# Up projection in seven products of block sums for five of eight pairs of k-tiles, on normalised x

## The chip, the cores and the metric

The kernel runs on one core of one Trainium2 chip. The metric is the time on the device in microseconds (us) of one execution; lower is better. Three runs of the kernel before were timed.

## What is computed

One layer of a sequence model on x of 256 tokens by 2048 features, all in float32: a mixing part (attention and a recurrence, with its own projections w_in and w_out), and after it an MLP:

```
h2 = rms_norm(x, norm_mlp[l])
u = jnp.square(jax.nn.relu(jnp.einsum('btd,df->btf', h2, mlp_up[l])))
x = x + jnp.einsum('btf,fd->btd', u, mlp_down[l])
```

mlp_up is 2048 by 8192, mlp_down 8192 by 2048. rms_norm divides each token's row by the root of its mean square and multiplies by norm_mlp.

## The kernel before, in words

**Numbers.** TensorE multiplies in a reduced form of float32 (fp32r). To keep float32's accuracy each operand is split into a part `hi`, rounded to fp32r, and a part `lo`, the rest; a product is three matmuls: hi by hi, hi by lo, lo by hi. x is the stationary operand (a unit `u[:, 0]` holds hi, `u[:, 1]` lo, four k-tiles of 128 features by 256 tokens), the weights stream.

**Jobs.** Weights come in jobs of 256 rows (two k-tiles) by 512 columns, listed in `jobs` (lines 478 to 496) in the order of use. `load` (499) fetches a job to one of NRAW = 4 raw tiles through SyncE's queue. `split` (514) takes the next raw tile, has ScalarE copy it to `hi` and VectorE subtract to `lo` (three buffers each, LOOK + 1), and loads another. It runs two jobs ahead of the matmuls. `gemm` (528) goes over the jobs of one group of 512 output columns: for each job two k-tiles by two halves of 128 tokens by three matmuls of 128 rows, 128 columns of weights and 512 columns, 12 matmuls, into one PSUM bank per half; then `evac` empties the banks. Banks have two tags, "acc" and "side", of four each; up and down groups take turns between them (529).

**MLP.** `up_group` (1386) makes 512 of the 8192 hidden columns, from 8 jobs, on `hT`, which is x times norm_mlp, not yet divided by the root mean square. Its evacuation `f` (1389) does that by a scale of 1/rms per token (`rstd2`), with the relu, in 32 pieces of 32 tokens by 128, which it moves to a tile `z` in 32-blocks: EV = (8, 8) says that eight of 16 pieces of each half go to ScalarE and the others to VectorE. `fin` (1402), which is called a job or so into the next group, transposes z by blocks on VectorE, squares and rounds on ScalarE, and subtracts on VectorE: the unit of u. A down group takes the eight k-tiles of two units and 512 output columns (four jobs, 48 matmuls); `add_evac` (1342) adds it to x in two additions. `make_h` (1359) makes hT from x as it stands after w_out; `first_stats` (1425) the scale.

**Order.** Lines 1428 to 1438: up groups 0 and 1; then for each e from 0 to 7 up group 2e + 2, four down groups on units 2e and 2e + 1, up group 2e + 3 (at e = 6 both up groups come first, at e = 7 none is left). Work of the kernel is recorded, not issued: a planner (`plan`, 193) sorts the recorded operations by its own costs and dependences, gives each engine its fixed order, and takes, of what can start earliest, the one with the lowest rank; splits have their rank lowered by SPL = 120. `hooks` put recorded work between the jobs of a group. All tiles of 1040 elements a partition share NF = 18 slots of tag "f"; units have eight slots of tag "act". As every operation is issued from line 332, the profile's groups are told apart by their tiles.

Of the kernel before, what the change touches and what calls it, by code (L numbers as in the profile page):

```python
# [21 lines left out]
P = 128  # L22
T = 256
# [8 lines left out]
NF = 18  # L32
NRAW = 4
LOOK = 2
EV = (8, 8)

SPL = 120
KEEP = 0.3
# [296 lines left out]
def record(ctx, tc, A, nc):  # L335
# [28 lines left out]
    def done(n=1):  # L364
        live[0] -= n
# [113 lines left out]
    cols = [(c + 512 * h, 512) for h in range(2) for c in (4096, 3072, 5120)] + [(c + 512 * h, 512) for h in range(2) for c in (0, 1024, 2048)]  # L479
    cols.insert(1, (6144, 288))  # L480
    for c0, n in cols:
        jobs += [(A["w_in"], 256 * k, c0, n) for k in range(8)]
    for hh in range(2):
        jobs += [(A["w_out"], r0 + 512 * hh + 256 * k, 512 * j, 512) for j in range(4) for r0 in (W, 0) for k in range(2)]
    def up_jobs(i):
        return [(A["up"], 256 * k, 512 * i, 512) for k in range(8)]
# [12 lines left out]
    def load(between=None):  # L499
# [14 lines left out]
    def split():  # L514
        if pos[1] < len(jobs):
            pos[1] += 1
            raw, n = raws.popleft()
            hi = wp.tile([P, 2, 512], F32R, tag="hi", bufs=LOOK + 1, name=nm("hi"))
            lo = wp.tile([P, 2, 512], F32R, tag="lo", bufs=LOOK + 1, name=nm("lo"))
            nc.rank = -SPL  # L520
            for ks in ((slice(0, 1), slice(1, 2)) if pos[1] < 4 else (slice(0, 2),)):
                nc.scalar.copy(hi[:, ks, :n], raw[:, ks, :n])
                nc.vector.tensor_sub(lo[:, ks, :n], raw[:, ks, :n], hi[:, ks, :n])
            parts.append((hi, lo))
            nc.rank = 0
            load()

    def gemm(units, w, c0, ncols, evac, side=False, hooks={}, off=0):
        turn[0] += w is w_up or w is w_dn
        acc = [bank("side" if turn[0] % 2 else "acc") for _ in range(2)]  # L530
        nu = 4 if w is not w_out and w is not w_dn else 2
        nh = 2 * nu
        for j in range(nh):
            assert jobs[pos[2]][0] is w and jobs[pos[2]][2:] == (c0, ncols)
            pos[2] += 1
            hi, lo = parts.popleft()
            split()
            if j in hooks:
                hooks[j]()
            if side:  # L540
                pump(BD * ncols / 512, BA * ncols / 512)
            for kk in range(2):
                k = 2 * j + kk
                u = units[off + j // 2]
                for t in range(2):
                    xh = u[:, 0, k % 4, t * P:(t + 1) * P]
                    xl = u[:, 1, k % 4, t * P:(t + 1) * P]
                    o = acc[t][:, :ncols]
                    nc.tensor.matmul(o, xh, hi[:, kk, :ncols], start=(k == 0), stop=False)
                    nc.tensor.matmul(o, xh, lo[:, kk, :ncols], start=False, stop=False)  # L550
                    nc.tensor.matmul(o, xl, hi[:, kk, :ncols], start=False, stop=(k == 2 * nh - 1))
        evac(acc)

    def rsqrt_small(out, ss, scale, bias):
# [801 lines left out]
    parts2 = cst.tile([P, 2, 4], F32, name="parts2")  # L1356
    rstd2 = cst.tile([P, 2], F32, name="rstd2")

    def make_h(j):
        u = unit("hT")  # L1360
        hT.append(u)
        if j < 3:
# [51 lines left out]
    def store_evac(j):  # L1414
        def f(acc):
# [113 lines left out]
```

## Time and profile before

| what | value |
|---|---|
| median of three runs | 1206.91 us (1206.66 to 1206.95) |
| the profiled execution | 1209.2 us, of which the span is 1207.1 us |
| TensorE matmul busy | 1197.7 us, 99%, 6062 matmuls |
| weight loads busy | 961.0 us, 80% |
| VectorE busy | 853.0 us, 71% |
| ScalarE busy | 736.5 us, 61% |
| DMA | 216.08 MB, mean 179 GB/s |

The span runs from the first to the last instruction of the program on the core. PE is TensorE's matmuls, PEld its weight loads, DVE VectorE, ACT ScalarE, SP SyncE. A matmul's end is modelled, so its length in the records (395 ns for 512 columns) is more than its distance to the next; the distance of starts is what a matmul costs in a row of them. In names, out<-in are tiles of the program; x<-x,acc is the residual addition of a down group, z<-side,rstd a piece of the relu.

### The profile page before, as it was taken

Reading aid. Unit: us, or ns where it says so; the run is one execution under the profiler, and the core shown is the slowest. Engines: PE = TensorE matmul, PEld = TensorE weight load, DVE = VectorE, ACT = ScalarE, POOL = GpSimd, SP = SyncE. Lnnn points to the kernel's source line nnn. Section 1 sums busy time; section 2 is a strip of 40 time slices with the busy share of each in tenths; the row PEclk is TensorE's granted clock in tenths of the full one; section 3 lists DMA queues with packets and bytes.
Section 4 is the critical chain, followed back from the end, with each engine's and each line's share of the span. In section 5 each row is a group of like instructions: output and inputs, shape, how many; then the busy total and the mean of one; then the engine's idle time right before and its main releaser. Section 6 shows DMA issues by size and latency. Waiting matters only on the chain.

```text
span 1207.1 us, 16430 instructions
## 1 busy us (share of the span) xinstructions
PE 1197.7 (99%) x6062; PEld 961.0 (80%) x6062; DVE 853.0 (71%) x1276; ACT 736.5 (61%) x1171; POOL 7.3 (1%) x31
## 2 busy tenths in 40 slices
PE   9999999999999999999999999999999999999998
PEld 6887887878777788788888888888888888888886
DVE  7789693996965966688558568568568568567754
ACT  7774566856597769876356356356356356367532
POOL 2000000000000000000000000000000000000000
PEclk9999999999999999999999999999999999999999
DMA  8655655446554445665665665665665655666563
GB/s 282 196 171 153 184 161 164 120 139 169 155 157 155 157 151 181 180 179 184 206 175 186 198 175 190 198 180 186 203 176 186 199 174 195 195 174 199 195 204 129
DMA packets 126287, 216.08 MB, mean 179 GB/s; under 512 B 21824, under 2 KB 24384, under 8 KB 126208
## 3 DMA queue, kind: packets, MB, share of 16 engines
q1 hardware_dynamic: 126208, 215.05, 58.8%
q8 instruction: 47, 0.77, 0.3%
q14 instruction: 32, 0.26, 0.1%
HBM read 211.09 MB, written 3.93 MB: 178 GB/s over the span
## 4 chain that ended last, share of the span: by engine, by line
PE 89%; ACT 4%; DVE 3%; issue 1%; DMA 1%; SPq 0%; ACTq 0%; DVEq 0%
PE acc L332 54%; PE side L332 29%; PE tr L332 2%; PE sm L332 2%; PE sm L177 2%; ACT hi L332 1%; DVE lo L332 1%; ACT z L332 1%; DMA raw<-w_in 1%; DMA x<-xt 0%; DVE v L332 0%; ACT junk L332 0%; DVE AR L332 0%; ACT gp L332 0%; ACT L332 0%
## 5 line engine op out<-in xcount | busy, mean ns | idle before, releaser
L332 DVE TENSOR_TENSOR lo<-raw,hi 128x1024 fp32r<-128x1024 f32 (+2 forms) x395 | 474.5, 1205 | 269.6 <-ACT hi L332 267.1
L332 ACT CAST hi<-raw 128x1024 fp32r<-128x1024 f32 (+2 forms) x395 | 407.4, 1034 | 332.4 <-PE acc L332 217.5
L332 PE MATMUL acc<-hi,xT 128*128 128x512 f32 (+1 forms) x832 | 266.9, 395 | 0.5 <-ACT hi L332 0.5
L332 PEld LDWEIGHTS acc<-hi,xT 128*128 128x128 f32 x832 | 153.8, 189 | 33.9 <-ACT hi L332 2.1
L332 PE MATMUL acc<-lo,xT 128*128 128x512 f32 (+1 forms) x416 | 163.7, 393 | 0.7 <-DVE lo L332 0.5
L332 PE MATMUL acc<-hi,u 128*128 128x512 f32 x512 | 163.4, 395 | 0.0
L332 PE MATMUL side<-hi,u 128*128 128x512 f32 x512 | 163.4, 395 | 0.0
L332 PE MATMUL side<-hi,hT 128*128 128x512 f32 x512 | 162.9, 396 | 0.5 <-DVE hT L332 0.3
L332 PE MATMUL acc<-hi,hT 128*128 128x512 f32 x512 | 162.1, 395 | 0.0
L332 PEld LDWEIGHTS side<-hi,hT 128*128 128x128 f32 x512 | 96.1, 188 | 24.6 <-DVE hT L332 0.7
L332 PEld LDWEIGHTS side<-hi,u 128*128 128x128 f32 x512 | 96.1, 188 | 23.4
L332 PEld LDWEIGHTS acc<-hi,hT 128*128 128x128 f32 x512 | 96.1, 188 | 23.3
L332 PEld LDWEIGHTS acc<-hi,u 128*128 128x128 f32 x512 | 96.1, 188 | 23.3
L332 PE MATMUL acc<-lo,hT 128*128 128x512 f32 x256 | 101.1, 395 | 0.0
L332 PE MATMUL acc<-lo,u 128*128 128x512 f32 x256 | 101.1, 395 | 0.0
L332 PE MATMUL side<-lo,u 128*128 128x512 f32 x256 | 101.1, 395 | 0.0
L332 PE MATMUL side<-lo,hT 128*128 128x512 f32 x256 | 101.1, 395 | 0.0
L332 PEld LDWEIGHTS acc<-lo,xT 128*128 128x128 f32 x416 | 78.6, 189 | 18.7 <-DVE lo L332 3.1
L332 ACT ACTIVATE z<-acc,rstd 32x128 f32<-32x128 f32 x128 | 45.9, 358 | 20.1 <-DVE z L332 10.2
L332 ACT ACTIVATE z<-side,rstd 32x128 f32<-32x128 f32 x128 | 45.9, 359 | 20.1 <-DVE z L332 10.2
L332 PEld LDWEIGHTS acc<-lo,u 128*128 128x128 f32 x256 | 48.1, 188 | 11.7
L332 PEld LDWEIGHTS acc<-lo,hT 128*128 128x128 f32 x256 | 48.1, 188 | 11.7
(249 smaller groups left out, 1210.0 us busy)
## 6 DMA issues: line engine op xcount, KB each, us to landing
raw<-up SPq DMA_DIRECT2D x128, 512.0 KB, 3.8
raw<-down SPq DMA_DIRECT2D x128, 512.0 KB, 4.3
raw<-w_in SPq DMA_DIRECT2D x93, 512.0 KB, 3.8
raw<-w_out SPq DMA_DIRECT2D x32, 512.0 KB, 3.9
raw<-w_in SPq DMA_DIRECT2D x8, 288.0 KB, 3.2
x<-x SPq DMA_DIRECT2D x4, 512.0 KB, 7.5
out<-x SPq DMA_DIRECT2D x8, 256.0 KB, 3.4
raw<-w_in SPq DMA_DIRECT2D x6, 256.0 KB, 5.2
```

Of the source, the lines that this page charges most:

```text
L177: p.fn(*p.args, **p.kw)
L332: op.fn(*op.args, **op.kw)
```

## The change

For two by two blocks of matrices, seven products of sums of blocks do the work of eight (Winograd's form). The blocks here are, for a pair of k-tiles, x as two halves of tokens by two k-tiles and the weights as two k-tiles by two halves of 256 columns. In up groups 3 to 15, jobs 1, 2, 4, 5 and 7 of eight (FAST, QUICK) become fast jobs:

- Weights: `split` leaves out the lo of one block that no product uses, makes four differences of blocks T (tile `T`) on VectorE, their hi `Th` on ScalarE and their lo `Tl` on VectorE.
- x: `normal_h` makes `hN`, x times norm_mlp times 1/rms, in place of hT for groups 2 to 15, and for each of the five pairs four sums of its blocks, `S`, with hi and lo. `rstd_rows` spreads 1/rms over the partitions: two diagonal tiles and one fp32 matmul by ones.
- Matmuls: `seven` issues seven products of three matmuls of 256 columns, into four banks in place of two; the other three jobs of the group add to the first two of them.
- Evacuation: `join` adds up the four banks to a tile `C` (one copy on ScalarE, seven additions on VectorE); the relu reads C, without a scale from group 2 on. EV = 13 gives 13 of 16 pieces of each half to ScalarE.
- Order: up group 2e + 2, two down groups, up group 2e + 3, two down groups.

```diff
-EV = (8, 8)
+EV = 13
+FAST = (1, 2, 4, 5, 7)
+QUICK = 3
...
+    allone = ones[:, :1].broadcast_to([P, P])
...
+    def fast(job):
+        return job[0] is w_up and job[2] >= 512 * QUICK and job[1] // 256 in FAST
     jobs += up_jobs(0) + up_jobs(1)
     for e in range(8):
-        if e < 7:
-            jobs += up_jobs(2 * e + 2)
-        if e == 6:
-            jobs += up_jobs(15)
-        jobs += [(A["down"], e * 1024 + 256 * k, 512 * j, 512) for j in range(4) for k in range(4)]
-        if e < 6:
-            jobs += up_jobs(2 * e + 3)
+        for j in range(4):
+            if e < 7 and not j % 2:
+                jobs += up_jobs(2 * e + 2 + j // 2)
+            jobs += [(w_dn, e * 1024 + 256 * k, 512 * j, 512) for k in range(4)]
...
+                if not fast(jobs[pos[1] - 1]):
+                    nc.vector.tensor_sub(lo[:, ks, :n], raw[:, ks, :n], hi[:, ks, :n])
             parts.append((hi, lo))
+            if fast(jobs[pos[1] - 1]):
+                Tr, Th, Tl = ftile([P, 4, 256], "T"), ftile([P, 4, 256], "Th", F32R), ftile([P, 4, 256], "Tl", F32R)
+                b = raw.rearrange("p k (n c) -> p k n c", n=2)
+                nc.vector.tensor_sub(Tr[:, 0:2], b[:, :, 1], b[:, 0])
+                nc.vector.tensor_sub(Tr[:, 2], b[:, 1, 1], Tr[:, 0])
+                nc.vector.tensor_sub(Tr[:, 3], b[:, 1, 0], Tr[:, 2])
+                nc.vector.tensor_sub(lo[:, 0, :256], raw[:, 0, :256], hi[:, 0, :256])
+                nc.vector.tensor_sub(lo[:, 1], raw[:, 1], hi[:, 1])
+                nc.scalar.copy(Th, Tr)
+                nc.vector.tensor_sub(Tl, Tr, Th)
+                done()
+                parts[-1] += (Th, Tl)
...
+    def seven(acc, u, k, S, B, first, last):
+        hi, lo, Th, Tl = B
+        lt, rt = slice(0, 256), slice(256, 512)
+        def a(t, kk):
+            return [u[:, i, k + kk, t * P:(t + 1) * P] for i in range(2)]
+        def s(i):
+            return [S[:, j, i] for j in range(2)]
+        def b(kk, n):
+            return [x[:, kk, n * 256:n * 256 + 256] for x in (hi, lo)]
+        def t(i):
+            return [x[:, i] for x in (Th, Tl)]
+        for n, half, x, y in ((2, lt, a(0, 0), b(0, 0)), (0, lt, a(0, 1), b(1, 0)), (0, rt, s(3), b(1, 1)), (3, lt, s(0), t(0)),
+                              (3, rt, s(2), t(1)), (2, rt, s(1), t(2)), (1, lt, a(1, 1), t(3))):
+            o = acc[n][:, half]
+            begin = first and n > 1 and half == lt
+            end = last and (n == 1 or half == rt)
+            nc.tensor.matmul(o, x[0], y[0], start=begin, stop=False, skip_group_check=True)
+            nc.tensor.matmul(o, x[0], y[1], start=False, stop=False, skip_group_check=True)
+            nc.tensor.matmul(o, x[1], y[0], start=False, stop=end, skip_group_check=True)
...
+        quick = [j for j in range(8) if fast((w, 256 * j, c0))]
+        acc = [bank("side" if turn[0] % 2 else "acc") for _ in range(4 if quick else 2)]
...
+            if j in quick:
+                seven(acc, units[j // 2], 2 * j % 4, sums_[FAST.index(j)], (hi, lo, *T_), j == quick[0], j == quick[-1])
+                done(2)
+                continue
...
+            if keep is not None:
+                nc.scalar.copy(keep[:, 2 * kp:2 * kp + 2], b.rearrange("p (k t) -> p k t", t=T))
...
+    def rstd_rows():
+        row_rstd(rstd2, parts2)
+        dg = ftile([P, 2, P], "diag")
+        for t in range(2):
+            nc.vector.tensor_scalar(dg[:, t], ident, rstd2[:, t:t + 1], None, op0=ALU.mult)
+        b = bank("tr")
+        nc.tensor.matmul(b[:, :T], allone, dg.rearrange("p t q -> p (t q)"), start=True, stop=True)
+        done()
+        r = ftile([P, T], "r2")
+        nc.scalar.copy(r, b[:, :T])
+        rows2.append(r)
+    def normal_h(j):
+        u, a = unit("hN"), hA[j]
+        hN.append(u)
+        for kk in range(4):
+            nc.vector.scalar_tensor_tensor(a[:, kk], a[:, kk], pc("g_mlp", 4 * j + kk), rows2[0], op0=ALU.mult, op1=ALU.mult)
+        nc.scalar.copy(u[:, 0], a)
+        nc.vector.tensor_sub(u[:, 1], a, u[:, 0])
+        for p in range(2):
+            if 2 * j + p in FAST:
+                S, sr = ftile([P, 2, 4, P], "S", F32R), ftile([P, 4, P], "sr")
+                a1, a2 = a[:, 2 * p], a[:, 2 * p + 1]
+                nc.vector.tensor_add(sr[:, 0], a1[:, P:], a2[:, P:])
+                nc.vector.tensor_sub(sr[:, 1], sr[:, 0], a1[:, :P])
+                nc.vector.tensor_sub(sr[:, 2], a1[:, :P], a1[:, P:])
+                nc.vector.tensor_sub(sr[:, 3], a2[:, :P], sr[:, 1])
+                nc.scalar.copy(S[:, 0], sr)
+                nc.vector.tensor_sub(S[:, 1], sr, S[:, 0])
+                sums_.append(S)
...
+        def join(acc):
+            C, q = ftile([P, 2, 512], "C"), ftile([P, 3, 256], "q")
+            lt, rt = slice(0, 256), slice(256, 512)
+            b0, b1, b2, b3 = acc
+            nc.scalar.copy(q[:, 0], b2[:, lt])
+            nc.vector.tensor_add(q[:, 2], q[:, 0], b2[:, rt])
+            nc.vector.tensor_add(q[:, 1], q[:, 2], b3[:, lt])
+            qf = q.rearrange("p a c -> p (a c)")
+            nc.vector.tensor_add(C[:, 0], qf[:, :512], b0)
+            nc.vector.tensor_add(C[:, 1, lt], q[:, 2], b1[:, lt])
+            nc.vector.tensor_add(C[:, 1, rt], q[:, 1], b1[:, rt])
+            nc.vector.tensor_add(C[:, 1, lt], C[:, 1, lt], b3[:, rt])
+            nc.vector.tensor_add(C[:, 1, rt], C[:, 1, rt], b3[:, rt])
...
+            C = join(acc) if i >= QUICK else None
             for t in range(2):
                 for tb in range(4):
                     rows = slice(32 * tb, 32 * tb + 32)
-                    src = acc[t].rearrange("p (f c i) -> p f c i", c=4, i=32)
+                    src = (C[:, t] if C is not None else acc[t]).rearrange("p (f c i) -> p f c i", c=4, i=32)
                     for cb in range(4):
-                        o, r = z[32 * cb:32 * cb + 32, :, t, tb, :], rstd2[rows, t:t + 1]
-                        if 4 * tb + cb < EV[t]:
-                            nc.scalar.activation(o, src[rows, :, cb, :], AF.Relu, scale=r)
+                        o, s = z[32 * cb:32 * cb + 32, :, t, tb, :], src[rows, :, cb, :]
+                        r = rstd2[rows, t:t + 1]
+                        if 4 * tb + cb < EV:
+                            nc.scalar.activation(o, s, AF.Relu, **({} if i > 1 else dict(scale=r)))
+                        elif i > 1:
+                            nc.vector.tensor_scalar(o, s, 0.0, None, op0=ALU.max)
                         else:
-                            nc.vector.tensor_scalar(o, src[rows, :, cb, :], r, 0.0, op0=ALU.mult, op1=ALU.max)
+                            nc.vector.tensor_scalar(o, s, r, 0.0, op0=ALU.mult, op1=ALU.max)
...
-        gemm(hT, w_up, 512 * i, 512, f, hooks=hooks)
+        gemm(hN if i > 1 else hT, w_up, 512 * i, 512, f, hooks=hooks)
...
-    def first_stats():
-        row_rstd(rstd2, parts2)
-    up_group(0, {2: lambda: make_h(3), 4: first_stats})
-    up_group(1, {1: fin_hook})
+    up_group(0, {2: lambda: make_h(3), 4: rstd_rows})
+    up_group(1, {2 * j: lambda j=j: normal_h(j) for j in range(4)})
+    done()
     for e in range(8):
-        if e < 7:
-            up_group(2 * e + 2, {1: fin_hook})
-        if e == 6:
-            up_group(15, {1: fin_hook})
         for j in range(4):
+            if e < 7 and not j % 2:
+                up_group(2 * e + 2 + j // 2, {1: fin_hook})
             gemm(us, w_dn, 512 * j, 512, store_evac(j) if e == 7 else add_evac(x2[j]), hooks={1: fin_hook}, off=2 * e)
-        if e < 6:
-            up_group(2 * e + 3, {1: fin_hook})
```

## Rows read from the trace of the kernel before

**Rows 1.** The page's parts 1 and 2: busy time, TensorE's granted clock

```profile
PE 1197.7 (99%) x6062; PEld 961.0 (80%) x6062; DVE 853.0 (71%) x1276; ACT 736.5 (61%) x1171; POOL 7.3 (1%) x31
...
PEclk9999999999999999999999999999999999999999
```

**Rows 2.** The chain that ended last, in order of time: start us, us, what

```profile
598.12 22.40 PE acc L332 x96
...
642.92 11.20 PE acc L332 x48
```

**Rows 3.** By stretch: us, PE, PEld, DVE, ACT, POOL busy; clock, DMA, GB/s

```profile
609.32:698.92 89.60, 89.60 (x386) 72.08 (x385) 59.53 (x76) 48.75 (x68) 0.00 (x0) 1.00 0.62 188
```

**Rows 4.** VectorE in order of time, with [idle before <- releaser]

```profile
503.24 0.16 DVE L332 TENSOR_TENSOR rstd<-rsq,rsv 128x2 f32<-128x2 f32 x1
...
602.04 1.23 DVE L332 TENSOR_TENSOR lo<-raw,hi 128x1024 fp32r<-128x1024 f32 x1 [1.57 <-ACT hi L332]
```

**Rows 5.** TensorE in order of time: eight 256-column matmuls, first and last

```profile
63.25 0.28 PE L332 MATMUL tr<-XA,DA 128*128 128x256 f32 x1
...
64.08 0.28 PE L332 MATMUL tr<-XAL,DA 128*128 128x256 f32 x1
```

**Rows 6.** Groups of weight loads: busy us, mean ns | idle before

```profile
L332 PEld LDWEIGHTS acc<-hi,hT 128*128 128x128 f32 x512 | 96.1, 188 | 23.3
```

**Rows 7.** Groups of TensorE, by form: an fp32 product

```profile
L332 PE MATMUL sm<-k,q 64*128 64x256 f32 x32 | 8.9, 408 | 0.0
```

**Rows 8.** Groups of VectorE, by form

```profile
L332 DVE TENSOR_TENSOR lo<-raw,hi 128x1024 fp32r<-128x1024 f32 x381 | 464.3, 1222 | 264.7 <-ACT hi L332 262.2
...
L332 DVE TENSOR_SCALAR z<-side,rstd 32x128 f32<-32x128 f32 x128 | 45.1, 352 | 12.7 <-ACT z L332 10.6
...
L332 DVE TENSOR_TENSOR x<-x,side 128x512 f32<-128x512 f32 x32 | 20.5, 681 | 0.0
L332 DVE STREAM_TRANSPOSE uf<-z 128x1024 f32<-128x1024 f32 x16 | 19.9, 1242 | 0.3
L332 DVE TENSOR_TENSOR u<-uf,u 128x1024 fp32r<-128x1024 f32 x16 | 19.6, 1222 | 9.9 <-ACT u L332 9.9
...
L332 DVE TENSOR_TENSOR S<-S,sm 128x256 f32<-128x256 f32 x4 | 1.7, 422 | 9.3 <-ACT junk L332 6.3 <-PE sm L177 3.0
```

**Rows 9.** VectorE in order of time: pairs and fours back to back

```profile
49.23 0.76 DVE L332 TENSOR_TENSOR lat<-pad 128x256 f32<-128x256 f32 x2
...
211.04 0.42 DVE L332 TENSOR_TENSOR S<-S,sm 128x256 f32<-128x256 f32 x1 [1.45 <-PE sm L177]
211.50 0.42 DVE L332 TENSOR_TENSOR S<-S,gc 128x256 f32<-128x256 f32 x1
...
497.23 1.67 DVE L332 SCALAR_TENSOR_TENSOR hT<-zt,con,hT 128x256 fp32r<-128x256 f32 x4
...
586.38 1.28 DVE L332 TENSOR_TENSOR x<-x,acc 128x512 f32<-128x512 f32 x2
...
638.53 2.35 DVE L332 TENSOR_TENSOR lo<-raw,hi 128x1024 fp32r<-128x1024 f32 x2
```

**Rows 10.** Who waited for whom, VectorE: us in total, times, longest us

```profile
DVE z L332 <- ACT z L332: 21.1, 48, 0.6
DVE u L332 <- ACT u L332: 9.9, 9, 1.1
```

**Rows 11.** Groups of ScalarE, by form

```profile
L332 ACT CAST hi<-raw 128x1024 fp32r<-128x1024 f32 x381 | 398.4, 1048 | 327.6 <-PE acc L332 214.3 <-PE side L332 85.9 <-issue 14.1
L332 ACT ACTIVATE z<-side,rstd 32x128 f32<-32x128 f32 x128 | 45.9, 359 | 20.1 <-DVE z L332 10.2 <-PE side L332 8.4
...
L332 ACT ACTIVATE uf<-uf 128x1024 f32<-128x1024 f32 x16 | 17.0, 1063 | 41.9 <-DVE uf L332 41.9
```

**Rows 12.** ScalarE in order of time: evacuation of up group 0

```profile
507.86 0.73 ACT L332 ACTIVATE z<-side,rstd 32x128 f32<-32x128 f32 x2 [1.05 <-PE side L332]
...
524.31 1.05 ACT L332 CAST u<-uf 128x1024 fp32r<-128x1024 f32 x1
```

More of the change, by code (lines that the diff above doesn't have):

```diff
@@ L481, in record @@
     for c0, n in cols:
-        jobs += [(A["w_in"], 256 * k, c0, n) for k in range(8)]
+        jobs += [(w_in, 256 * k, c0, n) for k in range(8)]
     for hh in range(2):
-        jobs += [(A["w_out"], r0 + 512 * hh + 256 * k, 512 * j, 512) for j in range(4) for r0 in (W, 0) for k in range(2)]
+        jobs += [(w_out, r0 + 512 * hh + 256 * k, 512 * j, 512) for j in range(4) for r0 in (W, 0) for k in range(2)]
     def up_jobs(i):
-        return [(A["up"], 256 * k, 512 * i, 512) for k in range(8)]
+        return [(w_up, 256 * k, 512 * i, 512) for k in range(8)]
+    def fast(job):
+        return job[0] is w_up and job[2] >= 512 * QUICK and job[1] // 256 in FAST
     jobs += up_jobs(0) + up_jobs(1)
     for e in range(8):
-        if e < 7:
-            jobs += up_jobs(2 * e + 2)
-        if e == 6:
-            jobs += up_jobs(15)
-        jobs += [(A["down"], e * 1024 + 256 * k, 512 * j, 512) for j in range(4) for k in range(4)]
-        if e < 6:
-            jobs += up_jobs(2 * e + 3)
+        for j in range(4):
+            if e < 7 and not j % 2:
+                jobs += up_jobs(2 * e + 2 + j // 2)
+            jobs += [(w_dn, e * 1024 + 256 * k, 512 * j, 512) for k in range(4)]
     raws, parts = deque(), deque()
@@ L522, in split @@
                 nc.scalar.copy(hi[:, ks, :n], raw[:, ks, :n])
-                nc.vector.tensor_sub(lo[:, ks, :n], raw[:, ks, :n], hi[:, ks, :n])
+                if not fast(jobs[pos[1] - 1]):
+                    nc.vector.tensor_sub(lo[:, ks, :n], raw[:, ks, :n], hi[:, ks, :n])
             parts.append((hi, lo))
+            if fast(jobs[pos[1] - 1]):
[10 more added lines that the diff above has]
+                parts[-1] += (Th, Tl)
@@ L528, in gemm @@
     def gemm(units, w, c0, ncols, evac, side=False, hooks={}, off=0):
         turn[0] += w is w_up or w is w_dn
-        acc = [bank("side" if turn[0] % 2 else "acc") for _ in range(2)]
+        quick = [j for j in range(8) if fast((w, 256 * j, c0))]
+        acc = [bank("side" if turn[0] % 2 else "acc") for _ in range(4 if quick else 2)]
         nu = 4 if w is not w_out and w is not w_dn else 2
@@ L535, in gemm @@
             pos[2] += 1
-            hi, lo = parts.popleft()
+            hi, lo, *T_ = parts.popleft()
             split()
@@ L548, in gemm @@
                     o = acc[t][:, :ncols]
-                    nc.tensor.matmul(o, xh, hi[:, kk, :ncols], start=(k == 0), stop=False)
-                    nc.tensor.matmul(o, xh, lo[:, kk, :ncols], start=False, stop=False)
-                    nc.tensor.matmul(o, xl, hi[:, kk, :ncols], start=False, stop=(k == 2 * nh - 1))
+                    more = dict(skip_group_check=True) if quick else {}
+                    nc.tensor.matmul(o, xh, hi[:, kk, :ncols], start=(k == 0), stop=False, **more)
+                    nc.tensor.matmul(o, xh, lo[:, kk, :ncols], start=False, stop=False, **more)
+                    nc.tensor.matmul(o, xl, hi[:, kk, :ncols], start=False, stop=(k == 2 * nh - 1), **more)
         evac(acc)
@@ L568, in tr, with to_unit @@
         nc.tensor.transpose(out, in_, ident[:k, :k])
-    def to_unit(u, xj, gname, j, fill=(0, 0)):
+    def to_unit(u, xj, gname, j, fill=(0, 0), keep=None):
         for kp in range(2):
@@ L1357, in record @@
     rstd2 = cst.tile([P, 2], F32, name="rstd2")
+    hA, hN, sums_ = [], [], []
     def make_h(j):
@@ L1372, in make_h @@
                 nc.vector.scalar_tensor_tensor(u[:, 1, kk, :], zt[:, kk], g, u[:, 0, kk, :], op0=ALU.mult, op1=ALU.subtract)
-            done(2)
+            done()
         else:
-            to_unit(u, x2[j], "g_mlp", j)
+            zt = ftile([P, 4, T], "zt")
+            to_unit(u, x2[j], "g_mlp", j, keep=zt)
+        hA.append(zt)
         squares(x2[j], parts2, j)
+    rows2 = []
+    def rstd_rows():
[27 more added lines that the diff above has]
+                sums_.append(S)
+                done()
+        done()
     for j in range(4):
@@ L1386, in up_group @@
     def up_group(i, hooks):
+        def join(acc):
[11 more added lines that the diff above has]
+            nc.vector.tensor_add(C[:, 1, rt], C[:, 1, rt], b3[:, rt])
+            done()
+            return C
         def f(acc):
             z = ftile([P, 4, 2, 4, 32], "z")
+            C = join(acc) if i >= QUICK else None
             for t in range(2):
@@ L1393, in f @@
                     rows = slice(32 * tb, 32 * tb + 32)
-                    src = acc[t].rearrange("p (f c i) -> p f c i", c=4, i=32)
+                    src = (C[:, t] if C is not None else acc[t]).rearrange("p (f c i) -> p f c i", c=4, i=32)
                     for cb in range(4):
-                        o, r = z[32 * cb:32 * cb + 32, :, t, tb, :], rstd2[rows, t:t + 1]
-                        if 4 * tb + cb < EV[t]:
-                            nc.scalar.activation(o, src[rows, :, cb, :], AF.Relu, scale=r)
-                        else:
-                            nc.vector.tensor_scalar(o, src[rows, :, cb, :], r, 0.0, op0=ALU.mult, op1=ALU.max)
+                        o, s = z[32 * cb:32 * cb + 32, :, t, tb, :], src[rows, :, cb, :]
[4 more added lines that the diff above has]
+                            nc.vector.tensor_scalar(o, s, 0.0, None, op0=ALU.max)
+                        else:
+                            nc.vector.tensor_scalar(o, s, r, 0.0, op0=ALU.mult, op1=ALU.max)
+            if C is not None:
+                done()
             def fin():
```

1 line of the change is left out of this document (added).

## The prediction

> **What bounds it now.** I read the page first: TensorE is busy 99% of the span at full granted clock in every slice [rows 1]. The chain of waits in order of time says where that decides: through the MLP it is nothing but TensorE, 22.40 us for each up group of 96 matmuls and 11.20 us for each down group of 48 [rows 2]. So one matmul of 512 columns costs 0.2333 us, and one pair of k-tiles (12 of them; I call it a job) 2.80 us. The table by stretch shows one whole turn of the loop over e (two up groups, four down groups, 32 jobs, 89.60 us): TensorE full, VectorE 59.5 us, ScalarE 48.8 us, DMA share 0.62 [rows 3]. VectorE waits 1.57 us before the split of an ordinary job [rows 4]: it is paced by TensorE through the three hi/lo buffers, not the reverse. Whatever shortens TensorE's stream shortens the run until VectorE, at 66%, becomes the pace.
>
> **What the change takes from TensorE.** Up groups 3 to 15 are 13 groups with five fast jobs each: 65 jobs. A fast job issues 7 products x 3 = 21 matmuls of 256 columns in place of 12 of 512. What a 256-column matmul with its own 128x128 weights costs back to back stands in the timeline: eight in a row start from 63.25 to 64.08 us, 0.83/7 = 0.1186 us apart [rows 5]. So 21 x 0.1186 = 2.491 us for 2.80 us: 0.309 us saved a job, **65 x 0.309 = 20.1 us**. A half turn (one up group, two down groups) goes from 44.8 to 5 x 2.491 + 11 x 2.80 = 43.3 us.
>
> The rows also show the danger here: a load of weights is 188 ns long in the records [rows 6], longer than the matmul it would hide behind, and the change adds 9 loads a job. But in the same eight matmuls each had its own load of the same size and kept the 0.119 us spacing, so loads overlap each other, and I add nothing; the bound from above is 188 ns each (a rival). [...]
>
> One matmul is added: the fp32 broadcast of rstd, 128x256. The nearest row is a 64x256 fp32 product, 8.9 us for 32, 0.28 us each [rows 7]; bounds 0 and some 2 us if TensorE waits for its operand in order. I take **+0.3 us**.
>
> **What it gives VectorE.** Durations from [rows 8]: 1024 elements 1.222 us, 512 0.681, 256 0.422. Back to back without a dependence the starts are closer: two of 1024 take 2.35, so 1.13 each; two of 512 take 1.28, so 0.60; two of 256 take 0.76, so 0.34; where the second needs the first, 256 costs 0.46 (211.04 to 211.50) [rows 9].
> - A fast job: the first two differences T in one instruction of 512 elements, which the next needs at once (0.60 + 0.12 = 0.72), two of 256 (0.46 + 0.34), lo in two parts (0.34 + 0.60), Tl 1.13: 3.59 us in place of 1.13. By full durations 3.85.
> - Each join: seven adds, 0.46 + 0.46 + 0.60 + 4 x 0.34 = 2.9 us (3.2 by durations).
> - Relu: 6 pieces where there were 16. I keep 0.352 us each, though the source is now SBUF for the fast groups: 2.1 us.
> - As before in each half turn: 11 ordinary splits 12.4, transpose and subtraction of u 2.3, four residual adds 2.4.
> Sum of a half turn: 18.0 + 2.9 + 2.1 + 12.4 + 2.3 + 2.4 = **40.1 us by starts, 43.2 by durations**, against TensorE's 43.3. The same sum by durations for a turn of before gives 39.1 + 11.3 + 4.9 + 5.4 = 60.7, against 59.5 in [rows 3], so the accounting holds. I take starts, since [rows 9] shows them for just these sizes. [...]
>
> To this come waits that don't vanish: VectorE's z for ScalarE's z, 21.1 us over 16 groups, and u for ScalarE, 9.9 us [rows 10]: 1.9 us a half turn. New is Tl, which waits for ScalarE's Th: 1.05 us of copy [rows 11] with 0.94 us of lo beside it, so 0.1 us plus two hand-overs, 0 to 0.4 us for five jobs, 0 to 2 us, of which the next job's differences can fill some. VectorE then needs 42.0 to 44.0 us where TensorE needs 43.3. Its load is uneven too: during the up group 5 x 3.59 + 3 x 1.13 + 1.2 of residual adds = 22.5 us against TensorE's 20.9; the 1.6 us, and the Tl waits, must come out of the two jobs' lead that the three hi/lo buffers allow (some 5 us), filled again in the down groups. Between 0 and 0.7 us of TensorE waiting a half turn I take 0.3, nearer to the low end since today's waits all lie under TensorE: **+3.9 us** for 13.
>
> **ScalarE** in a half turn: 16 hi and 5 Th copies of 1.05, 26 z of 0.36, one copy of 256, two passes over u: 22.0 + 9.4 + 0.4 + 2.1 = 34 of 43.3 us [rows 11]. It hides under TensorE, but z now takes turns: 13 pieces on ScalarE, three on VectorE, twice.
>
> **Normalising x.** rstd is ready at 503.40 us [rows 4]; group 0 is evacuated from 507.86 [rows 12]; the fourth tile of hN is first read by the seventh job of group 2, 22.4 + 6 x 2.80 = 39.2 us after that, at 547. In these 43.7 us VectorE owes 16 splits (18 us), six z pieces (2) and, in the order recorded, four tiles of four products (1.67 us [rows 9]) and a subtraction, 2.8 each, and for four of the five fast pairs four adds and a subtraction, 2.8 each, ahead of it: 22.4. Sum 42.5: the cover leaves 1 us, and its nine waits for ScalarE's copies lie in it. Bounds 0 and 9 x 0.4 = 4 us; I take **+1.0 us**, once.
>
> **The rest, at nothing, with its cover.** Four PSUM banks for a fast group: the next user of the tag is two groups on, 11.2 us, and the join frees them in some 4 us. Three more f tiles a job: of 18 slots nine hold x2 and S, nine are left for three jobs' T, Th, Tl; too few would delay the differences, and is part of the 0 to 0.7. The raw tiles are read longer, so SP's queue of 512 KB loads is let go later, but each has about ten us until its turn. Finer alternation moves no TensorE work; only the last u is nearer its use: from the last up group's end 22.4 + 5.6 = 28 us remain. Today that chain takes from 507.86 to 525.36 us, plus the subtraction, about 19 us [rows 12], and join and longer turns add some 6. It fits, barely.
>
> **Sum.** 20.1 - 0.3 - 3.9 - 1.0 = 14.9 us off. The profiled execution has 1209.2 us (span 1207.1 and 2.1 around it); the median of the runs is 1206.9. The saving is the same against either: **1192.0 us**.
>
> **Rivals.**
> - *VectorE shares the pace.* For it: 40.1 + 1.9 + 2 = 44.0 us is more than 43.3, the three-buffer lead is short, the order is fixed. Against: fillable waits. 0.7 x 13 = 9.1 us given back in place of 3.9: 1197 us.
> - *VectorE sets the pace and the run is slower.* Place: the half turns with a fast group. Price: full durations, 43.2, with 1.9 us of waits and 5 x 0.1 for Th: 45.6 us against 44.8 before, 13 x 0.8 = +10.4: 1217 us (the saving is gone with it). It decides from 44.8 us on. For it: dependent pairs pay 0.46 where free ones pay 0.34, and lo, z and T alternate with ScalarE. Against: [rows 9].
> - *Weight loads don't overlap at 256 columns.* [...] Here the change would not do what it says: seven products would cost more than eight.
> - *One late piece*, x by its 4 us or the last u: 3 us more, 1195 us.
>
> **Chances.** Forecast 0.58, shared pace 0.25, slower pace 0.13, weights 0.01, one late piece 0.03. A measurement of this kernel can tell about 0.2%, 2.4 us, from no change. The forecast's own range is 1185.5 (no waits, and 0.001 us less for each of 1365 matmuls, which two decimals leave open) to 1196. Over all it reaches into the shared pace: 1185.5 to 1206.0. Faster 0.83, within 0.2% 0.04 (a pace of 44.5 to 45 us), slower 0.13.
>
> **What would show it.** In the changed profile: starts of 256-column matmuls 0.119 us apart in the fast jobs; an up group of 20.9 us in the chain and 11.20 us for a down group; VectorE busy near 87% (853 + 65 x 2.63 + 13 x 3.2 - 160 x 0.352 + 25 = 1035 us of 1190) and ScalarE near 74% (736.5 + 65 x 1.05 + 160 x 0.36 + 13 x 0.4 + 9 = 877) [rows 1]; VectorE still waiting for hi with the releaser TensorE behind it. Wrong would be: up groups over 22 us, idle of TensorE put down to VectorE's Tl, lo or C, or a chain that runs through VectorE; or loads 0.19 us apart.

## The result, and the profile after

The changed kernel took 1192.23 us (median of 4 runs, 1191.58 to 1192.87), the kernel before beside it 1206.79 (4 runs, 1206.61 to 1206.95): a ratio of 0.9879, 95% interval 0.9862 to 0.9897, 14.6 us less. Forecast were 1192.0 us and 14.9 us less.

The page's parts 1 and 2 of the changed kernel, against [rows 1]:

```profile
PE 1179.4 (99%) x6649; PEld 979.9 (82%) x6649; DVE 974.1 (82%) x1579; ACT 844.8 (71%) x1421; POOL 7.3 (1%) x31
...
DVE  7789594896975976798988988988988998898864
...
PEclk9999999999999999999999999999999999999999
```

TensorE issues 587 matmuls more (65 x 9 = 585 for the fast jobs, the rest for the broadcast) and is busy 18 us less; VectorE goes from 71% to 82%, and in the MLP, from the eighteenth slice on, stands at 80% or more until near the end. The granted clock (PEclk) stands at 90% or more of full speed in every slice. The chain in order of time (start us, us, what), against [rows 2]:

```profile
621.06 20.89 PE side L334 x141
641.95 11.15 PE acc L334 x48
653.10 11.15 PE side L334 x48
664.25 20.96 PE acc L334 x141
```

A fast up group takes 20.9 us for 22.40, and in these rows the chain is TensorE alone, as in eight of the 13 fast groups. In the other five it goes back through VectorE. In the group that starts at 750.59 us:

```profile
751.80 1.14 DVE u L334
...
762.05 1.20 DVE x L334 x2
763.76 1.23 DVE Tl L334
...
765.04 6.82 PE acc L334 x44
```

The page's part 4 gives VectorE 10% of the span on the chain, for 3% before. On it lie u's subtraction and two residual additions (x), the work of other groups, ahead of the Tl of a fast job.

The matmuls of a fast job in order of time, on TensorE:

```profile
667.60 0.28 PE L334 MATMUL acc<-hi,S 128*128 128x256 f32 x1
...
668.07 0.28 PE L334 MATMUL acc<-Tl,S 128*128 128x256 f32 x1
...
669.37 0.29 PE L334 MATMUL acc<-hi,hN 128*128 128x256 f32 x1
```

Fifteen steps lie between the first and the last row: 1.77 / 15 = 0.118 us each, as in [rows 5], though each loads weights of its own. The same half turn by stretch (columns as in [rows 3]), and then the last fast group:

```profile
837.39:880.66 43.27, 43.27 (x239) 37.36 (x237) 38.46 (x61) 31.45 (x51) 0.00 (x0) 1.00 0.63 194
...
1097.49:1119.12 21.63, 21.10 (x142) 19.31 (x141) 21.07 (x34) 14.37 (x16) 0.00 (x0) 1.00 0.67 197
```

VectorE works 38.5 of 43.3 us where it worked 29.8 of 44.8 before (half of the turn in [rows 3]), and in the last fast group 21.07 of 21.63: there TensorE is idle for half a microsecond by the records. Who waits for whom (us in total, times, longest us), first TensorE, then VectorE:

```profile
PE acc L334 <- DVE lo L334: 1.0, 2, 0.6
PE acc L334 <- DVE Tl L334: 0.7, 2, 0.5
PE acc L334 <- ACT hi L334: 0.6, 1, 0.6
...
DVE lo L334 <- ACT hi L334: 148.7, 142, 4.4
...
DVE z L334 <- ACT z L334: 1.8, 5, 0.7
...
DVE u L334 <- ACT u L334: 1.1, 1, 1.1
```

VectorE still waits for hi; its waits for ScalarE's z and u are nearly gone, 1.8 and 1.1 us for 21.1 and 9.9 in [rows 10]. TensorE's waits are mostly too short for this list. They come out of group lengths, and so does the whole account, by the starts of the groups in the two profiled executions:

| part of the span | before, us | after, us | difference |
|---|---|---|---|
| up to the first MLP matmul | 484.07 | 484.71 | +0.6 |
| up groups 0 and 1 (the broadcast among them) | 46.69 | 47.05 | +0.4 |
| up group 2 | 22.40 | 22.31 | -0.1 |
| up groups 3 to 15, five fast jobs each | 291.2 | 275.0 | -16.2 |
| 32 down groups of 11.20, then 11.15 | 358.4 | 356.9 | -1.5 |

The sum is -16.8 (last matmul 1202.52, then 1185.82: -16.7). That is 2.1 us more than the medians differ, because the profiled execution of before lay 2.4 us over its median: in it a 512-column matmul took 0.2333 us, in that of after 0.2323, which is all there is to the last row and some 1.2 us of the row above it. The 0.6 us of the first row tell nothing: that start lies between 483.85 and 484.91 us in 11 of the 12 experiments, and at 486.34 in e11. At 0.2323 and 0.1182 us a fast group without waits takes 105 x 0.1182 + 36 x 0.2323 = 20.8 us, 13 of them 270.1; measured were 275.0, so TensorE waits 4.9 us in all, 1.3 of it in the first fast group (22.12 us) and 0.85 in the last. In the eleven between, the wait sits where the fourth fast job's Tl is used: Tl ends 4.2, 1.3, 0.8, 0.06 and 0.4 us ahead of its use for the five jobs of a typical group, and 0.06 is TensorE waiting for it.

### The profile page after: what moved, and what is told of

It is laid out like the page before. It is cut to its first block, busy times and chain, and to the rows that moved or that the text cites. A ratio compares the mean times of both kernels' runs of the same rounds, so it can differ in the third digit from the quotient of the medians.

```text
span 1190.2 us, 18141 instructions
## 1 busy us (share of the span) xinstructions
PE 1179.4 (99%) x6649; PEld 979.9 (82%) x6649; DVE 974.1 (82%) x1579; ACT 844.8 (71%) x1421; POOL 7.3 (1%) x31
## 4 chain that ended last, share of the span: by engine, by line
PE 77%; DVE 10%; ACT 7%; DMA 3%; issue 3%; SPq 0%; DVEq 0%; ACTq 0%
PE acc L334 47%; PE side L334 23%; DVE lo L334 4%; PE sm L334 3%; PE tr L334 3%; ACT z L334 2%; ACT hi L334 2%; DVE Tl L334 2%; DVE T L334 2%; PE sm L179 2%; DMA raw<-up 1%; DMA raw<-w_in 1%; DVE x L334 1%; DVE uf L334 0%; DVE u L334 0%
## 5 line engine op out<-in xcount | busy, mean ns | idle before, releaser
L334 DVE TENSOR_TENSOR lo<-raw,hi 128x1024 fp32r<-128x1024 f32 (+3 forms) x460 | 462.7, 1015 | 151.3 <-ACT hi L334 148.7
L334 ACT ACTIVATE z<-C 32x128 f32<-32x128 f32 x338 | 104.2, 308 | 39.4 <-DVE C L334 35.0
L334 ACT CAST Th<-T 128x1024 fp32r<-128x1024 f32 x65 | 68.2, 1050 | 71.0 <-DVE T L334 70.3
L334 PE MATMUL side<-hi,hN 128*128 128x512 f32 (+1 forms) x328 | 91.7, 353 | 0.0
L334 PE MATMUL acc<-hi,hN 128*128 128x512 f32 (+1 forms) x308 | 83.4, 343 | 0.0
L334 DVE TENSOR_TENSOR Tl<-T,Th 128x1024 fp32r<-128x1024 f32 x65 | 79.1, 1216 | 0.0
L334 PEld LDWEIGHTS side<-hi,hN 128*128 128x128 f32 x328 | 59.7, 188 | 9.5
L334 PEld LDWEIGHTS acc<-hi,hN 128*128 128x128 f32 x308 | 55.5, 188 | 7.8
L334 PE MATMUL side<-lo,hN 128*128 128x512 f32 (+1 forms) x164 | 57.9, 353 | 0.0
L334 PEld LDWEIGHTS side<-lo,u 128*128 128x128 f32 x256 | 48.2, 188 | 11.0
```

What stands on the lines that cost most here:

```text
L334: op.fn(*op.args, **op.kw)
```

## Experiments

My theory: the shorter matmuls bring all of the gain, VectorE has room as long as its work is spread, and what is lost are short waits for VectorE in the up groups. The rival: VectorE already sets the pace. The runs, each against the kernel before on the same chip (1206.66 us beside e1 to e4, 1208.35 beside e5 to e8, 1206.98 beside e9 to e11, 1206.89 beside e12). The differences in the text are to the changed kernel's 1192.23 us or between experiments, often across chips; as the medians of before differ by up to 1.7 us, one or two us are at the edge of what they tell (e3's 1.3 us, for one). The planner orders each kernel anew, so a small change can also move instructions that it doesn't name.

| run | us, median (lowest to highest) | ratio to before, 95% interval |
|---|---|---|
| e1_no_fast | 1207.31 (1206.69 to 1209.96) | 1.0009 (0.9999 to 1.002) |
| e2_dose_up | 1197.64 (1197.55 to 1197.75) | 0.9921 (0.99 to 0.9942) |
| e3_dose_down | 1193.55 (1192.88 to 1193.9) | 0.9886 (0.9869 to 0.9904) |
| e4_coarse | 1224.13 (1223.78 to 1224.73) | 1.0141 (1.0123 to 1.0159) |
| e5_ev8 | 1197.2 (1196.43 to 1199.34) | 0.9913 (0.9898 to 0.9928) |
| e6_six | 1203.89 (1202.22 to 1205.0) | 0.9965 (0.9952 to 0.9978) |
| e7_tail | 1202.55 (1201.81 to 1203.05) | 0.9954 (0.9939 to 0.9968) |
| e8_pool | 1281.67 (1278.65 to 1282.86) | 1.0605 (1.0584 to 1.0626) |
| e9_mix | 1189.89 (1189.61 to 1190.03) | 0.9856 (0.984 to 0.9873) |
| e10_mix_six | 1198.62 (1198.36 to 1199.57) | 0.993 (0.9915 to 0.9944) |
| e11_mix_dose | 1200.76 (1199.89 to 1202.78) | 0.9948 (0.9934 to 0.9963) |
| e12_mix_late_u | 1190.02 (1189.66 to 1192.06) | 0.9855 (0.9832 to 0.9878) |

**e1: everything but the fast jobs.** Eight products throughout, with the normalised x, the finer alternation and the new division of z kept.

```diff
-QUICK = 3
+QUICK = 16
```

> No up group is fast (all jobs take eight products); the normalised x, its sums, the finer order and 13 of 16 pieces on ScalarE stay. Theory (TensorE paces, all of the gain is the 21 shorter matmuls for 12): the gain is gone, 1207 us and a little, about +0.4 us for the broadcast matmul: 1206.8 to 1208. Rival (the order and the lighter VectorE bring part of the gain): 1200 to 1205.

No difference from before that the interval can tell from nothing (it ends at 0.2%, 2.4 us). So what the change does beside the seven products brings none of the gain; the 14.6 us are the shorter matmuls less their waits.

**e2 and e3: the same dose on VectorE in two places.** A 256-element subtraction of 0.33 us is repeated: in each fast job (65 times, 21.5 us), or in five of the eight jobs of the two down groups of a half turn (by the page's count of instructions 80 times, 26.4 us, since the three half turns without fast jobs get it too).

```diff
                 nc.vector.tensor_sub(lo[:, 0, :256], raw[:, 0, :256], hi[:, 0, :256])
+                nc.vector.tensor_sub(lo[:, 0, :256], raw[:, 0, :256], hi[:, 0, :256])
```

and in a down job, right behind its own lo:

```diff
+            if jobs[pos[1] - 1][0] is w_dn and (jobs[pos[1] - 1][2] // 512) % 2 * 4 + jobs[pos[1] - 1][1] // 256 % 4 < 5:
+                nc.vector.tensor_sub(lo[:, 0, :256], raw[:, 0, :256], hi[:, 0, :256])
```

> Each fast job repeats its subtraction of 256 elements on VectorE, 0.33 us by starts, 5 x 0.33 = 1.7 us in each of 13 up groups, 21.5 us in all. Theory (VectorE is full through the up group and its lead of two jobs is used up at the group's end, where the last fast job's Tl is already 0.1 to 0.8 us late): TensorE waits nearly all of it, 1208 to 1214 us. Rival (VectorE has 4.9 us idle a half turn and evens out over it): 1192 to 1195 us.

> The same repeated subtraction, five times a half turn, but in the splits of the down groups' jobs (five of eight). Theory (VectorE has 4 us idle there, and the place decides, not the sum): 1192 to 1194 us. Rival (VectorE's sum over the half turn sets the pace): as much as the dose in the up groups, 1208 to 1214 us.

In the down groups 1.3 of the 26.4 us come through, in the up groups 5.4 of 21.5. So VectorE's sum over the run doesn't decide, and the rival falls; the place does. But in the up groups three quarters were hidden too, where I had expected nearly all of it to show. TensorE's waits of e2:

```profile
PE acc L334 <- DVE Tl L334: 3.6, 9, 0.8
PE side L334 <- DVE Tl L334: 2.2, 6, 0.4
```

Tl, the last thing that VectorE makes for a fast job, is what comes late, again in the fourth fast job. The planner had moved other work too: one of the two residual additions that stand ahead of this Tl in the changed kernel stands behind it here.

**e4: the old order.** Two up groups in a row, then four down groups, as before the change; all else as after.

```diff
     for e in range(8):
+        if e < 7:
+            up_group(2 * e + 2, {1: fin_hook})
+        if e == 6:
+            up_group(15, {1: fin_hook})
         for j in range(4):
-            if e < 7 and not j % 2:
-                up_group(2 * e + 2 + j // 2, {1: fin_hook})
...
+        if e < 6:
+            up_group(2 * e + 3, {1: fin_hook})
```

(and the list of jobs in the same order). At e = 6 three up groups follow each other, as before the change.

> The fast jobs with the old order: two up groups, then four down groups. Theory (the finer alternation is what lets VectorE keep up): two up groups in a row ask VectorE for about 47 us in TensorE's 42, and the lead covers 1 to 2 of it: 3 to 5 us lost in each of 6 to 7 turns, 1212 to 1224 us, the gain gone. Rival (the order moves no work and costs nothing, as the prediction priced it): 1192 to 1194 us.

31.9 us slower than after, and 1.4% slower than before, with the same matmuls. By stretch, the first and the second up group of one turn:

```profile
689.92:710.69 20.77, 20.77 (x142) 19.16 (x141) 20.38 (x34) 12.39 (x13) 0.00 (x0) 1.00 0.67 216
710.69:737.10 26.41, 23.52 (x143) 20.70 (x142) 22.99 (x42) 22.26 (x42) 0.00 (x0) 0.94 0.43 141
```

The first is free of waits, the second takes 5.6 us more. Its waits in the whole run, and ScalarE in order of time within that stretch:

```profile
PE side L334 <- ACT hi L334: 13.2, 12, 1.7
PE side L334 <- DVE lo L334: 3.8, 6, 1.1
```

```profile
722.70 3.19 ACT L334 ACTIVATE z<-C 32x128 f32<-32x128 f32 x10
725.91 1.05 ACT L334 CAST hi<-raw 128x1024 fp32r<-128x1024 f32 x1
726.98 4.46 ACT L334 ACTIVATE z<-C 32x128 f32<-32x128 f32 x14
731.46 1.04 ACT L334 CAST hi<-raw 128x1024 fp32r<-128x1024 f32 x1
```

While the second group runs, the first one's evacuation (26 pieces of z on ScalarE, joins and transposes on VectorE) falls between the Th copies and the differences of its fast jobs. ScalarE runs 10 and 14 pieces in a row ahead of hi, and TensorE first waits for ScalarE, not for VectorE as I had written. The granted clock is lower too: 0.94 over that stretch, 1.00 over the first. The 13 pieces on ScalarE belong to the finer order, and e4 keeps them: what the old order would cost with eight was not run.

**e5: eight pieces of z on ScalarE in place of 13.** VectorE gets five pieces more for each half group.

```diff
-EV = 13
+EV = 8
```

> Eight of 16 relu pieces to ScalarE again, ten pieces more for VectorE in each half turn, 0.22 us each, 2.2 us, nearly all of it while the down groups run; ScalarE is relieved by ten pieces of 0.31. Theory (the place decides: VectorE has 4 us idle in the down groups): 1192 to 1195 us. Rival (VectorE's sum sets the pace): half of the dose or more, 1206 us and over.

Slower by 5 us, but not where I looked: all 13 fast groups run at 20.76 to 20.90 us, with no wait, though VectorE has 38 us more to do. The loss is one wait, between up group 2 and the first down group, on TensorE in order of time, and the clock around it by stretch:

```profile
553.62 0.40 PE L334 MATMUL side<-hi,hN 128*128 128x512 f32 x1
560.13 0.80 PE L334 MATMUL acc<-hi,u 128*128 128x512 f32 x1 [6.12 <-ACT u L334]
```

```profile
553.60:560.10 6.50, 0.42 (x2) 0.00 (x0) 5.99 (x13) 5.32 (x8) 0.00 (x0) 0.85 0.26 92
560.10:562.40 2.30, 2.07 (x4) 1.16 (x4) 2.30 (x3) 2.13 (x8) 0.00 (x0) 0.50 0.67 226
```

The u of group 0 is 6.1 us late. Its z are done by 523 us, but in VectorE's order its transposition stands behind the normalising of x, which ends at 548.80 us, and nine z of group 1, and starts at 554.70 us (in the changed kernel at 544.78). When TensorE resumes, its granted clock is 0.50 over the 2.30 us of the second row, and 512-column matmuls start 0.42 to 0.43 us apart (from 560.73 to 561.15 and 561.58 us); from 565.10 to 565.34 us it is 0.24 again. This is the forecast's "one late piece", brought on by the setting.

**e6 and e7: a sixth fast job; the fifth one moved ahead.**

```diff
-FAST = (1, 2, 4, 5, 7)
+FAST = (1, 2, 4, 5, 6, 7)
...
-FAST = (1, 2, 4, 5, 7)
+FAST = (1, 2, 4, 5, 6)
```

> A sixth fast pair (1, 2, 4, 5, 6, 7): TensorE saves another 13 x 0.31 = 4.0 us, VectorE gets 2.2 us more in each up group. Theory (VectorE enters the up group with a lead that is nearly used up; the dose of 1.7 us a group already let 0.4 us through, and what comes on top goes through in full): 2.5 - 1.3 = 1.2 us a group, +16 - 4, about 1204 us. First rival (it goes through by a quarter, as the dose did): +8 - 4, 1196 us. Second rival (VectorE has room): 1188 us.

> Fast pairs 1, 2, 4, 5, 6 in place of 1, 2, 4, 5, 7: the same work, but an ordinary job ends each group. Theory (TensorE waits at the last fast job's Tl because VectorE's lead has run out there, 0.1 to 0.8 us a group; an ordinary job at the end gives no lead back ahead of job 6): the wait moves to job 6 and stays or grows, 1192 to 1195 us. Rival (the wait belongs to the end of the group): it goes, 1188 to 1190 us.

The sixth job should give 13 x 0.31 = 4.0 us and costs 11.7, as the theory had it (1204 us); e7 has the work of after and costs 10.3 us. TensorE's waits in e7:

```profile
PE acc L334 <- DVE Tl L334: 5.7, 9, 1.4
PE side L334 <- DVE Tl L334: 3.6, 6, 0.8
```

Three fast jobs in a row are what hurts: the wait moves to job 6's Tl, 0.8 us a group. I read from this that the ordinary job between the fast ones is where VectorE regains its lead. The size was beyond what I gave it in e7.

**e8: the differences on GpSimd.** The three subtractions that make T move off VectorE.

```diff
-                nc.vector.tensor_sub(Tr[:, 0:2], b[:, :, 1], b[:, 0])
+                nc.gpsimd.tensor_sub(Tr[:, 0:2], b[:, :, 1], b[:, 0])
```

(and the other two alike).

> The three difference instructions of a fast job go to GpSimd, which is idle: VectorE loses 1.26 us a job, 6.3 us an up group. Theory (all that TensorE still waits for in the up groups, some 4 us over the whole run, is VectorE's work): 1187 to 1190 us, if GpSimd makes a job's differences in under about 4 us. Rival (GpSimd is slow at this, or slows VectorE beside it): T late, TensorE waits for Tl, 1195 us and over.

89 us slower than after. TensorE waits 46.3 us for VectorE's lo, VectorE 56.1 us for ScalarE's Th, and ScalarE 172.8 us for GpSimd's T. Groups by form, first GpSimd's, then one of VectorE's in this run:

```profile
L334 POOL TENSOR_TENSOR T<-raw,T 128x256 f32<-128x256 f32 x130 | 161.4, 1242 | 10.2
...
L334 DVE TENSOR_TENSOR lo<-raw,hi 128x256 fp32r<-128x256 f32 x65 | 61.1, 940 | 0.0
```

and the same two of the changed kernel, where VectorE does both:

```profile
L334 DVE TENSOR_TENSOR T<-raw,T 128x256 f32<-128x256 f32 x130 | 54.3, 418 | 0.4
...
L334 DVE TENSOR_TENSOR lo<-raw,hi 128x256 fp32r<-128x256 f32 x65 | 27.1, 417 | 0.0
```

GpSimd takes 1.24 us for what VectorE does in 0.42, and VectorE's own lo goes from 0.42 to 0.94 us with it.

**e9: EV by group.** 13 where x is being normalised, 8 from group 2 on. This puts e5's one wait to the test as well.

```diff
-                        if 4 * tb + cb < EV:
+                        if 4 * tb + cb < (EV if i < 2 else 8):
```

> 13 of 16 relu pieces to ScalarE for up groups 0 and 1, where VectorE also normalises x, and eight of 16 from group 2 on. Theory (with 13, the long run of pieces on ScalarE ends u so late that its subtraction on VectorE, 1.13 us, falls into the next up group, where VectorE is full; with eight it falls 4 us ahead of it; the 6.5 us wait of the run with eight throughout is u of group 1 alone): fast groups of 20.8 us and no wait for u, 1188 to 1190 us, below both kernels. Rival (what the eight pieces gave the up groups they take back elsewhere): 1192 us or more.

1189.89 us: the lowest of all these kernels, 17 us below before and 2.3 us below the changed one. The intervals of the two ratios overlap, so for the 2.3 us the trace has to speak. By stretch, a half turn:

```profile
836.00:879.00 43.00, 43.00 (x238) 37.05 (x237) 40.59 (x71) 28.38 (x41) 0.00 (x0) 1.00 0.61 195
```

VectorE is busy 94% of it and TensorE never waits; the fast groups take 20.75 to 20.85 us but for the first (21.97), and from the second on their chain is TensorE alone. More work on VectorE, and fewer waits for it. The wait of e5 for u is gone with the 13 pieces in groups 0 and 1.

**e10 and e11: is there room now?** The sixth fast job, or the dose of e2, on top of e9.

```diff
-FAST = (1, 2, 4, 5, 7)
+FAST = (1, 2, 4, 5, 6, 7)
```

```diff
                 nc.vector.tensor_sub(lo[:, 0, :256], raw[:, 0, :256], hi[:, 0, :256])
+                nc.vector.tensor_sub(lo[:, 0, :256], raw[:, 0, :256], hi[:, 0, :256])
```

> The same with a sixth fast pair. Theory (u's subtraction out of the up group leaves VectorE 1.1 us more there; the sixth pair asks 2.2 + 0.3, of which some 1.3 was covered before): 0.1 to 0.3 us of waiting a group, 1185 to 1189 us. Rival (VectorE's own work is the limit, wherever u falls): the sixth pair costs what it did, 0.9 us a group, 1199 to 1202 us.

> The same with five fast pairs and the dose of 1.7 us in each up group (the repeated subtraction of 256 elements in each fast job). Theory (room of 1.1 us was made): the dose lets less through than the 0.42 us a group that it let through before, 1189 to 1193 us. Rival (the room is not there): 5 us as before, 1194 to 1196 us.

There is too little: +8.7 us and +10.9 us over e9. Of the dose, 5 x 0.33 = 1.65 us a fast group, 10.9 / 13 = 0.84 comes through, twice as much as beside EV = 13 (5.4 / 13 = 0.42). I had taken the lack of waits in e9 for room; neither theory allowed for so much. The trace of e9 had the size of the room: from the second fast group on, the Tl of the fifth fast job ends 0.2 to 1.0 us ahead of its use, 0.7 on average, and 1.65 - 0.7 is about one us. TensorE's waits in e11 are again for Tl, now in the fifth fast job:

```profile
PE acc L334 <- DVE Tl L334: 5.4, 9, 1.0
PE side L334 <- DVE Tl L334: 3.6, 6, 0.9
```

**e12: why are there waits with EV = 13?** With 13 pieces, VectorE's subtraction for u starts 0.9 to 2.1 us inside the next up group, with eight some 4.4 us ahead of it. Here e9 is given the late subtraction.

```diff
-                nc.vector.tensor_sub(u[:, 1], uf, u[:, 0])
-                done(2)
+                def sub():
+                    nc.vector.tensor_sub(u[:, 1], uf, u[:, 0])
+                    done()
+                done()
+                if 2 <= i < 15:
+                    late_u.append(sub)
+                else:
+                    sub()
...
+    def up_hook():
+        nc.hold = True
+        while late_u:
+            late_u.pop(0)()
+        nc.hold = False
+        fin_hook()
...
-                up_group(2 * e + 2 + j // 2, {1: fin_hook})
+                up_group(2 * e + 2 + j // 2, {1: up_hook})
```

> The kernel of the mixed 13 and eight pieces (1189.9 us, fast groups of 20.8 us), with one thing moved: the subtraction of u on VectorE, 1.13 us, is held back until the first jobs of the next up group, where the changed kernel has it. The work is the same. Theory (the changed kernel's waits of 0.1 to 0.4 us at the end of a fast group come from this piece falling into the group): the waits return, groups of 20.9 to 21.2 us, 1191 to 1194 us. Rival (the place of this piece is not the cause, as the dose that cost more beside eight pieces than beside 13 suggests): groups of 20.8 us, 1189 to 1190.5 us.

1190.02 us, as e9. But the piece is not where the changed kernel has it: it starts 12.6 to 14.7 us inside the up group, behind the Tl of the fourth fast job. On VectorE in order of time:

```profile
674.88 1.22 DVE L334 TENSOR_TENSOR Tl<-T,Th 128x1024 fp32r<-128x1024 f32 x1
...
676.62 1.22 DVE L334 TENSOR_TENSOR u<-uf,u 128x1024 fp32r<-128x1024 f32 x1
```

There it can delay only what follows, and in four of the 13 groups waits of 0.2 to 0.4 us come back, in the ordinary job behind it and at the last fast job's Tl. So e12 doesn't decide on my theory. What is seen is the lead at the fourth fast job, 0.06 us in the changed kernel and 1.2 to 2.0 us in e9 from the second fast group on, and what VectorE does ahead of that Tl within the group: in the changed kernel u's subtraction and two residual additions (on the chain above), in e9 one addition:

```profile
675.32 0.68 DVE L334 TENSOR_TENSOR x<-x,side 128x512 f32<-128x512 f32 x1
675.92 1.22 DVE L334 TENSOR_TENSOR Tl<-T,Th 128x1024 fp32r<-128x1024 f32 x1
677.05 0.69 DVE L334 TENSOR_TENSOR x<-x,side 128x512 f32<-128x512 f32 x1
```

That is 1.13 + 0.60 us of work of other groups more ahead of it. No run moved these alone, so which of them makes the waits **stays open**.

## Why the prediction was right, and where it was not

**What bounds the kernel, and the 0.309 us a job: right.** 0.118 us a matmul, 20.9 us an up group; e1 shows that nothing else brings the gain. With the measured steps a job saves 12 x 0.2323 - 21 x 0.1182 = 0.305 us, 19.9 us in all; less the waits of 4.9 and the 0.4 of groups 0 and 1 that is 14.6 us, as the medians have it; with the 0.6 us ahead of the MLP it would be 14.0. The rival on weight loads is out: a fast job has 9 more loads, each 188 to 190 ns long in the records of after, and its matmuls still start 0.118 us apart, as in [rows 5]. Loads that did not overlap would take 21 x 0.188 = 3.95 us a job, in place of 2.80.

**VectorE by starts, not by durations: right.** The durations of VectorE's instructions in e9's half turn add up to 44.5 us (70 instructions), in a stretch of 43.0 us in which VectorE also idles for 2.4 us: they overlap. The slower rival (45.6 us a half turn) and the shared pace (44.0) both fall, since the terms were too high; a half turn of the changed kernel kept VectorE busy for 38.5 us, where 40.1 were forecast by starts. Two of the forecast's signs of being wrong did show, in small: the first fast group took 22.12 us, and the chain runs through VectorE in five groups.
- A fast job: dependent differences at 0.46 us each. The order puts an independent subtraction, lo, between them, so the second costs 0.34. VectorE in order of time:

```profile
576.95 0.42 DVE L334 TENSOR_TENSOR T<-raw,T 128x256 f32<-128x256 f32 x1
577.29 1.02 DVE L334 TENSOR_TENSOR lo<-raw,hi 128x256 fp32r<-128x256 f32 x2
578.22 0.42 DVE L334 TENSOR_TENSOR T<-raw,T 128x256 f32<-128x256 f32 x1
```

  That makes 0.60 + 3 x 0.34 + 0.60 + 1.13 = 3.35 us in place of 3.59.
- z takes 0.222 us on VectorE in the fast groups, not the 0.352 that was kept. Two things changed there, the source (SBUF for PSUM) and the scale, which is gone. Up group 2 has the second without the first, at 0.295 us: some 0.06 us come from the scale, 0.07 from the source. The waits of 1.9 us a half turn that "don't vanish" did vanish. VectorE came out at 974 us for 1035, ScalarE at 845 for 877.

```profile
L334 DVE TENSOR_SCALAR z<-C 32x128 f32<-32x128 f32 x78 | 17.3, 222 | 1.7
...
L334 DVE TENSOR_SCALAR z<-side 32x128 f32<-32x128 f32 x6 | 1.8, 295 | 0.3 <-ACT z L334 0.2
```

**The waits, +3.9: about right in size (4.9), wrong in kind.** I spread 0.3 us over 13 half turns as VectorE running short. 2.2 of the 4.9 us are in the first and the last fast group, the rest at one place, the fourth fast job's Tl, and depends on the order more than on the load: e9 has more load and hardly any waits, e7 has the same load and 10 us more.

**Normalising x, +1.0: mis-sized.** The block sums are 128-element adds that start 0.2 us apart, so that a pair costs some 4 x 0.2 + 0.6 = 1.4 us, not 2.8. Up group 2 ran in 22.31 us without a wait: the term is 0. e5's first wait shows that the cover is thin all the same. Two such adds and the subtraction that ends a pair, on VectorE in order of time, in e5:

```profile
546.38 0.28 DVE L334 TENSOR_TENSOR sr<-sr,zt 128x128 f32<-128x128 f32 x1
546.58 0.28 DVE L334 TENSOR_TENSOR sr<-zt 128x128 f32<-128x128 f32 x1
...
548.12 0.68 DVE L334 TENSOR_TENSOR S<-sr,S 128x512 fp32r<-128x512 f32 x1
```

**The finer alternation, "moves no TensorE work": true, and the step that missed most.** I priced it at nothing and asked only whether the last u still fits. The gain hangs on it, with 13 pieces on ScalarE: e4 shows 31.9 us more without it, though without the fast jobs, in e1 and in the kernel before, the two orders give the same time. Where I did argue from place, in the two jobs' lead and the filling in the down groups, e2, e3, e6 and e7 bear it out: the down groups take a dose for next to nothing, a third fast job in a row does not fit.

**The broadcast, +0.3:** 0.36 measured, as the difference of up groups 0 and 1. So 14.9 against 14.6 rests in part on terms that offset each other: normalising 1.0 too high, waits 1.0 too low. That the number came out so close is in part luck.

## What to carry to other kernels

Work taken off the engine that bounds the run and given to a helper was paid here in the stretch where the helper is loaded, not in its average (5.4 us for the dose in the up groups, e2, and 1.3 us for a larger one in the down groups, e3): alternate heavy and light groups as finely as the data allow (e4: 31.9 us), and price the order of the work by running the new load in the old order. A repeated instruction, once in each stretch, shows in two runs where there is room; a helper without visible waits may still have too little (e11). How far its last product ends ahead of its use was the room here (0.7 us in e9). Divide work between helpers by stage, since the setting that suits the start (13) isn't the one for the rest (8): 1189.89 us with both, 1192.23 with 13 throughout, 1197.2 with eight.

## What the hardware showed unexpectedly

A 512-column matmul steps 0.2333 us in some half turns and 0.2323 in others of one execution (down groups of 11.20 and 11.15 us within e9), so that one profiled execution can't be compared with another below 0.4%. After TensorE's wait of 6.1 us in e5 the granted clock was 0.50 over 2.30 us, and in e4 it was 0.94 over an up group of 26.41 us in which TensorE was busy 23.52 us. A piece of z without the scale took VectorE 0.295 us out of PSUM and 0.222 out of SBUF, but ScalarE 0.268 out of PSUM and 0.308 out of SBUF. GpSimd's subtraction of 256 fp32 elements took 1.24 us, and with it VectorE's of the same size took 0.94 us, 0.52 us more than in the changed kernel (e8).
